# The first stage of a two-block kernel: input modulated before the tables, rounds one group ahead, products with an operand in PSUM

## The chip, the cores and the metric

The kernel runs on one core of one Trainium2 chip. A core has TensorE (matrix products), VectorE, ScalarE and GpSimd, which work side by side on 128 partitions, with SyncE starting transfers; the rows call them PE, DVE, ACT, POOL and SP. Data lies in SBUF, and matrix products are written to PSUM, which the other engines can read and VectorE and ScalarE here also write. The metric is the device time of one execution in microseconds (us); less is better.

## What is computed

Two transformer-like blocks with a model width of 1024 and a sequence of 512. Only the first mixer is touched by the change. It is a modulated RMS norm, a projection, a diagonal complex state space model in 64 groups of 16 channels with 64 states each, a gelu, a gated product and an output projection:

```
def s5_mixer(h, w_in, lam_re, lam_im, log_dt, b_re, b_im, c_re, c_im, d_skip, w_glu, w_out):
    u = h @ w_in                      # h: the modulated input, 512 x 1024
    dt = exp(log_dt); mag = exp(lre * dt)
    lb = mag * cos(lim * dt), mag * sin(lim * dt)          # the discrete eigenvalue
    k = (lb - 1) / lam                                     # k_re, k_im
    bb = k * b                                             # complex, 64 states x 16 channels per group
    h[l] = lb * h[l-1] + bb @ u[l]                         # a scan over 512 steps
    y = Re(c @ h) + d_skip * u
    y = gelu(y); y = y * sigmoid(y @ w_glu)
    return y @ w_out
```

Then come a gated FFN with a convolution, an attention with forgetting, another FFN, and in the second block a further attention, its FFN and a last attention.

## The kernel before

Every fp32 product of the large projections is made as three products of parts: operands are split in a high part (`hi`) and a low part (`lo`, the rest), and `mm3` (L373 to L375) adds hi by hi, lo by hi and hi by lo. So a product of one 128-wide output slice over the whole width is 8 x 3 = 24 matmuls of 128x512.

**The start of the first stage** (0 to about 78 us). RMS norm: sums of squares come from TensorE as they arrive, `norm.sums()` turns them into a reciprocal root by a short chain on VectorE (L206 to L261, then four products `dg` at L212), `norm.spread` broadcasts it by TensorE and `rs` takes it to SBUF. `normalise(k)` (L899) multiplies the eight slices of the input by it on GpSimd. Beside that VectorE works out cosine, sine and exponential for 64 x 64 eigenvalues (`sincos`, 62 instructions), `l1r, l1i`, then `k` (`kre`, `kim`, L822 to L834); GpSimd makes eight powers of the eigenvalue (`LR`, `LI`, L805 to L814); VectorE makes larger powers (`pows`, L857 to L861) and from these the table `few` (tile `cb`, L864 to L875). The modulation `A, B` (L1114, L416) needs a small product of TensorE, which ends with the last of 32 parts of the modulation's weights. `split_x(k)` makes the eight pairs of parts of the modulated input: `hnh` on ScalarE (L909), the whole value again (tile `t`, on VectorE for odd k by the mask `V_DVE`, L911, on ScalarE for even k, L913), and `hnl` as their difference on VectorE (L914).

**Eight groups** n = 0 to 7 (of eight 16-channel groups each) then go through steps whose order is written out by hand in the string `ORDER`. VectorE, TensorE and GpSimd run in just that order; ScalarE's order is set by the scheduler, by its own estimate of when operands are there. The steps:
- `K` tables: ScalarE scales two rows of the loaded `bc`, GpSimd makes `k1, k2` = k times b (six products of 128x128, L969 to L974)
- `F` the outer product `bt` of powers and k1, k2 (`for_b`, on VectorE, six instructions of 128x512, all operands in SBUF) and `C` the outer product `cp` of powers and c (`for_c`, on GpSimd, six of 128x576; the tile `cp` has three buffers)
- `W` split of an input weight slice (`whi` on ScalarE, `wlo` on GpSimd, 128x1024; two buffers) and `G` the 24 matmuls of the projection slice
- `P` eight transposes (L1015, into two PSUM tiles `pt`, copied by ScalarE to `bp`, L1016) and eight pairs of small products (L1022, L1025) that ScalarE copies to `lags`, from which the DMAs of `A` build a Toeplitz matrix
- `L` and `U` transfers (the group's input in another layout; the rotations `ecs`), `R` six products on VectorE that make a table of rotations from `few`
- `I` eight products of input and `bp`; `S` on VectorE two products, a sum, a scan and a product; `B` on VectorE a product and a sum; `O` 32 small products (L1080, L1082), which read `cp` too
- `Y`, `v`, `a`, `b`: the first of the gated products

The line that names the positions and the buffer that ties GpSimd to TensorE are

```
Z_POOL, W_ADD, SUMS_POS, SPREAD_POS, GATE_RATE = 0, 'dve', 12, 22, 1.3
self.cp = sp.tile([P, G8, 9, 16], F32, name="cp", bufs=3)
```

`SUMS_POS` and `SPREAD_POS` say behind how many of the 32 weight parts on TensorE the two steps of the norm stand. PSUM pools: `ps_s` three buffers, `ps_t` two, `ps_a` one.

## Time and profile before

| | us |
|---|---|
| median of three runs | 2670.97 |
| the runs | 2665.52, 2674.68, 2670.97 |
| the profiled execution | 2667.51 |
| its span | 2665.7 |
| TensorE busy | 2520.3 |
| VectorE busy | 1786.4 |
| ScalarE busy | 1149.9 |
| GpSimd busy | 408.0 |
| mean granted clock of TensorE | 0.968 |

The first stage takes the first 258 us of the span. A timeline row gives start, duration, engine, line and operation, `out<-in`, shape and count, and in brackets how long the engine stood idle just before and what released it. A windows row gives for a stretch its length and then, for TensorE, its weight loads, VectorE, ScalarE and GpSimd, the busy time with the number of instructions; then the granted TensorE clock (1.00 is 2.4 GHz, 0.50 is 1.2 GHz), the share of DMA and its rate.

### The profile page before, as it was taken

What the parts mean: (1) busy time and instruction counts of PE and PEld (TensorE: products, weight loads), DVE (VectorE), ACT (ScalarE), POOL (GpSimd) and SP (SyncE); (2) the same over time, 40 slices, a digit from 0 to 9 for tenths busy, and PEclk for the clock granted to TensorE, in tenths of its full rate; (3) what the DMA queues carried; (4) which work ended last, traced back from release to release, by engine and by line L of the source; (5) the groups of instructions that cost most, each with busy time, mean ns of one, the idle gap of its engine ahead of it and who ended that gap; (6) DMA issues with size and microseconds to landing.
All of it is one profiled execution on the core that took longest, in us unless ns stands there. A gap on an engine that the chain in (4) does not pass through costs nothing. (4 is left out here: it accounts for less than half of the span.)

```text
span 2665.7 us, 32804 instructions
## 1 busy us (share of the span) xinstructions
PE 2520.3 (95%) x12098; PEld 2021.3 (76%) x12098; DVE 1786.4 (67%) x3071; ACT 1149.9 (43%) x1915; POOL 408.0 (15%) x396
## 2 busy tenths in 40 slices
...
GB/s 200 110 125 150 229 191 139 136 149 120 105 112 103 111 121 163 155 171 179 143 103 115 115 95 127 162 149 172 170 139 98 32 29 95 83 87 99 101 77 75
DMA packets 131121, 335.67 MB, mean 126 GB/s; under 512 B 37009, under 2 KB 41873, under 8 KB 130961
## 3 DMA queue, kind: packets, MB, share of 16 engines
...
## 5 line engine op out<-in xcount | busy, mean ns | idle before, releaser
L267 DVE TENSOR_TENSOR wlo<-wraw,whi 128x1024 fp32r<-128x1024 f32 (+4 forms) x424 | 465.4, 1098 | 421.4 <-ACT whi L266 415.9
L266 ACT ACTIVATE whi<-wraw 128x1024 fp32r<-128x1024 f32 (+4 forms) x431 | 408.6, 949 | 759.6 <-PE mm L374 558.3
L373 PE MATMUL mm<-hnh,whi 128*128 128x512 f32 x1152 | 467.1, 406 | 39.1 <-ACT hnh L909 29.6
L374 PE MATMUL mm<-hnl,whi 128*128 128x512 f32 x1152 | 462.9, 402 | 6.3 <-POOL hnl L291 3.9
L375 PE MATMUL mm<-hnh,wlo 128*128 128x512 f32 x1152 | 459.1, 399 | 0.1
L373 PE MATMUL mm<-g,whi 128*128 128x512 f32 (+1 forms) x922 | 359.9, 391 | 6.3 <-ACT g L266 3.1
L375 PE MATMUL mm<-g,wlo 128*128 128x512 f32 (+1 forms) x922 | 359.3, 390 | 0.0
L374 PE MATMUL mm<-g,whi 128*128 128x512 f32 (+1 forms) x922 | 358.8, 389 | 0.1
L373 PEld LDWEIGHTS mm<-hnh,whi 128*128 128x128 f32 x1152 | 219.4, 191 | 90.9 <-ACT hnh L909 29.9
L373 PE MATMUL s<-hnh,whi 128*128 128x512 f32 x720 | 288.2, 400 | 0.0
L374 PE MATMUL s<-hnl,whi 128*128 128x512 f32 x720 | 285.2, 396 | 0.0
L375 PE MATMUL s<-hnh,wlo 128*128 128x512 f32 x720 | 283.8, 394 | 0.0
L374 PEld LDWEIGHTS mm<-hnl,whi 128*128 128x128 f32 x1152 | 219.0, 190 | 63.5 <-POOL hnl L291 9.2
L375 PEld LDWEIGHTS mm<-hnh,wlo 128*128 128x128 f32 x1152 | 218.8, 190 | 50.0 <-issue 0.7
L131 DVE SCALAR_TENSOR_TENSOR ada<-ada,cb 128x1024 f32<-128x1024 f32 x192 | 239.5, 1248 | 8.3 <-DMA ada<-in_ada_w_dram 8.1
L373 PEld LDWEIGHTS mm<-g,whi 128*128 128x128 f32 x922 | 173.6, 188 | 45.4 <-ACT g L266 3.8
L374 PEld LDWEIGHTS mm<-g,whi 128*128 128x128 f32 x922 | 173.9, 189 | 37.8 <-DVE g L272 0.7
L375 PEld LDWEIGHTS mm<-g,wlo 128*128 128x128 f32 x922 | 173.8, 189 | 37.6 <-issue 0.8
L375 PEld LDWEIGHTS s<-hnh,wlo 128*128 128x128 f32 x720 | 135.2, 188 | 32.7 <-issue 0.7
L373 PEld LDWEIGHTS s<-hnh,whi 128*128 128x128 f32 x720 | 135.4, 188 | 30.2
L374 PEld LDWEIGHTS s<-hnl,whi 128*128 128x128 f32 x720 | 135.4, 188 | 29.7 <-issue 0.5
L586 ACT ACTIVATE p<-p,nb 128x128 f32<-128x128 f32 x192 | 106.0, 554 | 69.9 <-DVE nb L581 41.7
...
## 6 DMA issues: line engine op xcount, KB each, us to landing
...
```

What stands on the lines that cost most here:

```text
L131: dve.scalar_tensor_tensor(raw, raw, 1.0, cb, op0=OP.mult, op1=OP.mult, accum_out=dst[:, i:i + 1])
L266: act.activation(hi, v, AF.Copy)
L267: return eng.tensor_tensor(lo, v, hi.bitcast(F32), OP.subtract)
L373: pe.matmul(ps, wh, xh, start=start, stop=False)
L374: pe.matmul(ps, wh, xl, start=False, stop=False)
L375: return pe.matmul(ps, wl, xh, start=False, stop=stop).ins
L586: act.activation(p[:, sl], p[:, sl], AF.Exp, bias=nb[:, qb:qb + 1], scale=scale, accum_out=l[:, qb:qb + 1])
```

## The change

Four things are changed, all in the first stage.
- **The start.** `SUMS_POS` goes from 12 to 8 and `norm.sums()` stands ahead of sincos on VectorE; `SPREAD_POS` from 22 to 18, and `spread`, `rs` and the eight `normalise` stand ahead of `l1r` and the powers. `split_x` for the first two slices and the first weight split stand right behind the modulation; the table `few` is merged with the other `split_x`; the first `F` and `R` are steps of `ORDER`, behind `G0`.
- **k folded into the powers.** `KR, KI` = powers times k (six instructions of 128x512 on GpSimd, once, with temporaries in the tile name `t0`) take the place of `k1, k2` in each group (six of 128x128 on GpSimd).
- **One operand in PSUM.** b is copied by ScalarE to a PSUM tile (`bsp`), and `for_b` reads it there: two instructions of 128x512 and eight of 128x256 instead of six of 128x512, and its temporary is in PSUM too. The powers for `few` and its temporary, and in `states` and `back` the second input, the sum, the scan and the swapped copy are in PSUM. The small products of `P` read `bt` for `k1`, and both their outputs are in `pt` tiles.
- **`ORDER`.** Steps are put in another order; rounds stand one group further ahead.

```
--- before.py
+++ after.py
@@ -71,12 +71,17 @@
 C_DVE, BC_BUFS = 0, 3
-Z_POOL, W_ADD, SUMS_POS, SPREAD_POS, GATE_RATE = 0, 'dve', 12, 22, 1.3
+Z_POOL, W_ADD, SUMS_POS, SPREAD_POS, GATE_RATE = 0, 'dve', 8, 18, 1.3
 T_ACT, MERGE_AT = 0, 50
-ORDER = ("G0 K1 W1 G1 C1 P0 F1 U1 L0 I0 L1 W2 G2 W3 K2 S0 A0 F2 B0 C2 L2 R1 G3 P1 I1 O0 U2 A1 W4 K3 S1 F3 "
-         "B1 C3 L3 G4 P2 I2 O1 U3 A2 W5 K4 S2 F4 B2 C4 L4 G5 P3 I3 O2 R2 U4 A3 W6 K5 S3 F5 B3 C5 L5 P4 I4 "
-         "G6 O3 U5 A4 W7 K6 S4 F6 B4 C6 L6 G7 P5 I5 O4 R3 U6 A5 K7 S5 F7 B5 C7 L7 P6 I6 A6 P7 O5 U7 S6 B6 "
-         "I7 A7 O6 Y0 Y1 S7 B7 O7 v0 Y2 Y3 Y4 Y5 a0 a1 a2 a3 v1 a4 a5 b0 b1 b2 b3 b4 b5 Y6 Y7 a6 a7 b6 b7 ")
+ORDER = ("G0 W1 F0 G1 L0 R0 U0 P0 A0 K1 W2 C1 F1 G2 L1 I0 K2 "
+         "S0 F2 B0 U1 C2 W3 P1 A1 G3 I1 O0 R1 U2 L2 K3 "
+         "S1 F3 B1 C3 W4 P2 A2 G4 I2 O1 U3 L3 K4 "
+         "S2 F4 B2 C4 W5 P3 A3 G5 I3 O2 R2 U4 L4 K5 "
+         "S3 F5 B3 C5 W6 P4 A4 G6 I4 O3 U5 L5 K6 "
+         "S4 F6 B4 C6 W7 P5 A5 G7 I5 O4 R3 U6 L6 K7 "
+         "S5 F7 B5 C7 P6 A6 I6 O5 U7 L7 Y0 v0 Y1 "
+         "S6 Y2 B6 P7 A7 a0 a1 I7 O6 v1 Y3 "
+         "S7 Y4 B7 a2 a3 b0 b1 O7 Y5 b2 b3 a4 b4 a5 b5 Y6 Y7 a6 a7 b6 b7 ")
+
+        for i in range(BC_POS, SUMS_POS):
+            part(i)
+        act.dma_start(vec, ap["vecs"])
+        merge(ln.ops)
+        norm.sums()
...
+        for i in range(SUMS_POS, SPREAD_POS):
+            part(i)
+        rb = norm.spread(ps_mm, "mm")
+        rs = tmp.tile([P, S], F32, name="t3")
+        act.activation(rs, rb, AF.Copy)
+        hs = []
+
+        def normalise(k):
+            t = hnp.tile([P, S], F32, name="hnl")
+            pool.tensor_tensor(t, h[k], rs, OP.mult)
+            hs.append(t)
+        for k in range(KD):
+            normalise(k)
         l1r, l1i = sm("l1r"), sm("l1i")
         dve.tensor_tensor(l1r, mag, cs, OP.mult)
         dve.tensor_tensor(l1i, mag, sn, OP.mult)
...
+        KR, KI = (sc.tile([P, NG, 8], F32, name=n) for n in ("KR", "KI"))
         kre, kim, den, nre = sm("kre"), sm("kim"), sm("den"), sm("nre")
...
+        up = [ps_s.tile([P, S], F32, name="s") for _ in range(2)]
+        turn_by = [up[i // 2][:, i % 2 * 256:i % 2 * 256 + 192].rearrange("p (e g) -> p e g", e=3) for i in range(3)]
+        for x, y in zip(turn_by, pows):
+            act.activation(x, y, AF.Copy)
         few = cst.tile([P, D], F32, name="cb").rearrange("p (e g n) -> p e g n", e=2, n=8)
...
         X = []
...
@@ -955,44 +951,41 @@
                 if n == len(bcs):
                     bcs.append(load_bc(n))
                 self.bc = bc = bcs[n]
-                b1, b2, c1, c2 = (bc[:, j, :].rearrange("p (g c) -> p g c", c=16) for j in range(4))
-                self.c12 = c1, c2
-                act.activation(bc[:, 1, :], bc[:, 1, :], AF.Identity, scale=sgn[:, 1:2])
+                self.c12 = [bc[:, j, :].rearrange("p (g c) -> p g c", c=16) for j in (2, 3)]
                 act.activation(bc[:, 2, :], bc[:, 2, :], AF.Identity, scale=sgn[:, 0:1])
                 act.activation(bc[:, 3, :], bc[:, 3, :], AF.Copy, scale=-1.0)
-                sh = [P, G8, 16]
-                self.k1 = k1 = sp.tile(sh, F32, name="k1", bufs=3)
-                self.k2 = k2 = sp.tile(sh, F32, name="k2")
-                t = sp.tile(sh, F32, name="kt", bufs=1)
-                krb = kre[:, gs, None].to_broadcast(sh)
-                kib = kim[:, gs, None].to_broadcast(sh)
-                pool.tensor_tensor(k1, krb, b1, OP.mult)
-                pool.tensor_tensor(t, kib, b2, OP.mult)
-                pool.tensor_tensor(k1, k1, t, OP.add)
-                pool.tensor_tensor(k2, krb, b2, OP.mult)
-                pool.tensor_tensor(t, kib, b1, OP.mult)
-                pool.tensor_tensor(k2, k2, t, OP.subtract)
-
-            def outer(self, dst, x1, x2, re, im, eng, n, t):
-                half = [P, 4, n, 16]
...
+            def for_c(self, eng):
+                self.cp = cp = sp.tile([P, G8, 9, 16], F32, name="cp", bufs=3)
+                t = sp.tile([P, 4, 9, 16], F32, name="op", bufs=1)
+                x1, x2 = self.c12
+                half = [P, 4, 9, 16]
                     g0 = self.i * G8 + a
+                    lr, li = (x[:, g0:g0 + 4, :, None].to_broadcast(half) for x in (LR, LI))
+                    eng.tensor_tensor(cp[:, a:a + 4], lr, x1[:, a:a + 4, None, :].to_broadcast(half), OP.mult)
                     eng.tensor_tensor(t, li, x2[:, a:a + 4, None, :].to_broadcast(half), OP.mult)
-                    eng.tensor_tensor(dst[:, a:a + 4], dst[:, a:a + 4], t, OP.add)
+                    eng.tensor_tensor(cp[:, a:a + 4], cp[:, a:a + 4], t, OP.add)
 
             def for_b(self, eng):
 
-                self.bt = sp.tile([P, G8, 8, 16], F32, name="bt")
-                self.outer(self.bt, self.k1, self.k2, LR[:, :, 7::-1], LI[:, :, 7::-1], eng, 8,
+                self.bt = bt = sp.tile([P, G8, 8, 16], F32, name="bt")
+                x1, x2 = self.b12
+                half, quarter = [P, 4, 8, 16], [P, 2, 8, 16]
+                t = bsp[:, 256:512].rearrange("p (g a c) -> p g a c", g=2, a=8)
+                g0 = self.i * G8
+                for a in range(0, 8, 4):
+                    eng.tensor_tensor(bt[:, a:a + 4], KR[:, g0 + a:g0 + a + 4, ::-1, None].to_broadcast(half),
+                                      x1[:, a:a + 4, None, :].to_broadcast(half), OP.mult)
+                for a in range(0, 8, 2):
+                    eng.tensor_tensor(t, KI[:, g0 + a:g0 + a + 2, ::-1, None].to_broadcast(quarter),
+                                      x2[:, a:a + 2, None, :].to_broadcast(quarter), OP.mult)
+                    eng.tensor_tensor(bt[:, a:a + 2], bt[:, a:a + 2], t, OP.add)
...
                 self.lags = sp.tile([16, G8, P], F32, name="lags", bufs=LAG_BUFS)
                 for a in range(2):
-                    pk = (ps_t if a else ps_a).tile([16, 4, P], F32, name="pt" if a else "aux")
+                    pk = ps_t.tile([16, 4, P], F32, name="pt")
                     for g in range(4):
-                        pe.matmul(pk[:, g, :], self.k1[:, a * 4 + g, :],
+                        pe.matmul(pk[:, g, :], self.bt[:, a * 4 + g, 7, :],
                                   self.cp[:, a * 4 + g, 0:8, :].rearrange("p a b -> p (a b)"), start=True, stop=True)
                         c = slice((a * 4 + g) * 16, (a * 4 + g + 1) * 16)
                         pe.matmul(pk[:, g, 0:16], ident[:, 0:16], self.bc[:, 4, c], start=False, stop=True,
...
             sa = ps_s.tile([P, G8, 64], F32, name="s")
             for g in range(G8):
                 pe.matmul(sa[:, g, :], tab.bp[:, g, :], U[:, g, :], start=True, stop=True)
-            sb = tmp.tile([P, G8, 64], F32, name="t1")
+            sb = ps_s.tile([P, G8, 64], F32, name="s")
             for a in range(2):
                 act.activation(sb[HALF[a]], sa[HALF[1 - a]], AF.Copy)
             return sa, sb
@@ -1050,26 +1043,22 @@
 
             sa, sb = sab
             z0 = tmp.tile([P, G8, 64], F32, name="t0")
-            z1 = sb
             dve.tensor_mul(z0, sa, tab.ec)
-            dve.tensor_mul(z1, sb, tab.es)
-            (pool if Z_POOL else dve).tensor_tensor(z0, z0, z1, OP.add)
-            dve.tensor_tensor_scan(z1.rearrange("p a b -> p (a b)"), tab.d0.rearrange("p a b -> p (a b)"),
-                                   z0.rearrange("p a b -> p (a b)"), 0.0, OP.mult, OP.add)
-            zs = tmp.tile([P, G8, 64], F32, name="t2")
+            dve.tensor_mul(sb, sb, tab.es)
+            dve.tensor_tensor(sa, z0, sb, OP.add)
+            dve.tensor_tensor_scan(sa.rearrange("p a b -> p (a b)"), tab.d0.rearrange("p a b -> p (a b)"),
+                                   sa.rearrange("p a b -> p (a b)"), 0.0, OP.mult, OP.add)
             for a in range(2):
-                act.activation(zs[HALF[a]], z1[HALF[1 - a]], AF.Copy, scale=-1.0)
+                act.activation(sb[HALF[a]], sa[HALF[1 - a]], AF.Copy, scale=-1.0)
             w1 = tmp.tile([P, G8, 64], F32, name="t3")
-            dve.tensor_mul(w1, z1, tab.ec)
-            return w1, zs
+            dve.tensor_mul(w1, sa, tab.ec)
+            return w1, sb
 
         def back(tab, wz):
 
             w1, zs = wz
             dve.tensor_mul(zs, zs, tab.es)
-            if W_ADD == "pe":
-                return w1, zs
-            (pool if W_ADD == "pool" else dve).tensor_tensor(w1, w1, zs, OP.add)
+            dve.tensor_tensor(w1, w1, zs, OP.add)
             return w1,
...
         tabs, U = [], []
-
+        bsp = ps_a.tile([P, S], F32, name="aux")
         tabs.append(Tables(0))
-        for k in range(KD):
-            normalise(k)
-        lt, lc = Later(dve), Later(dve)
-        E[0] = rotations(0, lt)
-        tabs[0].for_b(lc)
-        if C_DVE & 1:
-            tabs[0].for_c(lc)
-        else:
-            tabs[0].for_c(pool)
-        n = len(lc.ops) * MERGE_AT // 100
-        merge(lt.ops, lc.ops[:n])
-        tabs[0].turns()
-        wt = split_w(0, pool if W_DVE & 256 else dve)
+        lf = Later(dve)
+        et = ps_s.tile([P, 2, NG, 4], F32, name="s")
+        lf.memset(few[:, 0, :, 0:1], 1.0)
+        lf.memset(few[:, 1, :, 0:1], 0.0)
...
+        for x, y, z, op in ((KR, kre, kim, OP.subtract), (KI, kim, kre, OP.add)):
+            sh = [P, NG, 8]
+            t = tmp.tile(sh, F32, name="t0")
+            pool.tensor_tensor(x, LR[:, :, 0:8], y[:, :, None].to_broadcast(sh), OP.mult)
+            pool.tensor_tensor(t, LI[:, :, 0:8], z[:, :, None].to_broadcast(sh), OP.mult)
+            pool.tensor_tensor(x, x, t, op)
         dve.tensor_tensor(mod00[:, 0:16].rearrange("p (j i) -> p j i", i=4), ada_ps[:, :, 0::32].rearrange("p i j -> p j i"),
                           col("ada_b", 0, 16).rearrange("p (j i) -> p j i", i=4), OP.add)
         A, B = affine(mod00, 0, 8, col("norm_g", 0, KD), "s5")
-        merge([lambda k=k: split_x(k) for k in range(KD)], lc.ops[n:])
+        split_x(0)
+        split_x(1)
+        wt = split_w(0, dve)
+        tabs[0].for_c(pool)
+        merge([lambda k=k: split_x(k) for k in range(2, KD)], lf.ops)
```

Where the order moved: GpSimd around the third `C`. Before (names carry buffer numbers; `wlo_975` is the low part of weight slice 4, `cp_1014` the fourth `cp`, of C3, whose buffer is that of the first):

```order
L267 TENSOR_TENSOR wlo_975<-wraw_770,whi_974 128x1024
L969 TENSOR_TENSOR k1_985<-sm_kre_304,bc_980 128x128
L970 TENSOR_TENSOR kt_987<-sm_kim_305,bc_980 128x128
L971 TENSOR_TENSOR k1_985<-k1_985,kt_987 128x128
L972 TENSOR_TENSOR k2_986<-sm_kre_304,bc_980 128x128
L973 TENSOR_TENSOR kt_987<-sm_kim_305,bc_980 128x128
L974 TENSOR_TENSOR k2_986<-k2_986,kt_987 128x128
L982 TENSOR_TENSOR cp_1014<-LR_120,bc_980 128x576
L983 TENSOR_TENSOR op_1015<-LI_121,bc_980 128x576
L984 TENSOR_TENSOR cp_1014<-cp_1014,op_1015 128x576
```

And GpSimd at the same place after (`wlo_850` is slice 3, `cp_1002` is C3, `wlo_1011` slice 4, `cp_1155` C4):

```order
L973 TENSOR_TENSOR cp_841<-cp_841,op_842 128x576
L272 TENSOR_TENSOR wlo_850<-wraw_639,whi_849 128x1024
L971 TENSOR_TENSOR cp_1002<-LR_120,bc_974 128x576
L972 TENSOR_TENSOR op_1003<-LI_121,bc_974 128x576
L973 TENSOR_TENSOR cp_1002<-cp_1002,op_1003 128x576
L971 TENSOR_TENSOR cp_1002<-LR_120,bc_974 128x576
L972 TENSOR_TENSOR op_1003<-LI_121,bc_974 128x576
L973 TENSOR_TENSOR cp_1002<-cp_1002,op_1003 128x576
L272 TENSOR_TENSOR wlo_1011<-wraw_746,whi_1010 128x1024
L971 TENSOR_TENSOR cp_1155<-LR_120,bc_1127 128x576
```

Before, the low part of slice 4 stands ahead of C3; after, it stands behind it, and so in each round from there on.

TensorE where it reads that low part, after (`pt_1040` is the last of P2, `mm_1058` is G4):

```order
L1015 MATMUL pt_1040<-cp_841,bt_823 16x128
L1018 MATMUL pt_1040<-bc_507,cc_87 16x16
L378 MATMUL mm_1058<-hnh_527,whi_1010 128x512
L379 MATMUL mm_1058<-hnl_528,whi_1010 128x512
L380 MATMUL mm_1058<-hnh_527,wlo_1011 128x512
```

The third matmul of G4 reads `wlo_1011`, and behind G4 stand I2 and O1. Before, I2 and O1 stood ahead of G5, which reads the low part that is made behind C3 (slice 5).

ScalarE at the modulated input, before (`t0_570` is the whole value of slice 0) and after (`t0_529` is that of slice 0, `t2_556` of slice 2; `hnl_361` and so on are the normalised slices):

```order
L909 ACTIVATE hnh_568<-hnl_517,m_ada00_132,A_s5_566 128x512
L913 ACTIVATE t0_570<-hnl_517,m_ada00_132,A_s5_566 128x512
L909 ACTIVATE hnh_575<-hnl_519,m_ada00_132,A_s5_566 128x512
L909 ACTIVATE hnh_581<-hnl_521,m_ada00_132,A_s5_566 128x512
L913 ACTIVATE t2_583<-hnl_521,m_ada00_132,A_s5_566 128x512
```

```order
L905 ACTIVATE hnh_563<-hnl_367,m_ada00_132,A_s5_525 128x512
L905 ACTIVATE hnh_572<-hnl_369,m_ada00_132,A_s5_525 128x512
L905 ACTIVATE hnh_581<-hnl_371,m_ada00_132,A_s5_525 128x512
L905 ACTIVATE hnh_590<-hnl_373,m_ada00_132,A_s5_525 128x512
L905 ACTIVATE hnh_599<-hnl_375,m_ada00_132,A_s5_525 128x512
L909 ACTIVATE t2_592<-hnl_373,m_ada00_132,A_s5_525 128x512
L909 ACTIVATE t0_529<-hnl_361,m_ada00_132,A_s5_525 128x512
L909 ACTIVATE t0_574<-hnl_369,m_ada00_132,A_s5_525 128x512
```

The whole value of slice 0 has moved from the second place to the tenth, behind all eight high parts and the whole value of slices 2 and 6. Beyond the first stage the instructions of all engines stand as before.

## Rows read from the trace of the kernel before

**Rows 1.** The page: busy time of each engine, share of the span, instructions.
```profile
PE 2520.3 (95%) x12098; PEld 2021.3 (76%) x12098; DVE 1786.4 (67%) x3071; ACT 1149.9 (43%) x1915; POOL 408.0 (15%) x396
```

**Rows 2.** Windows: three stretches of the first stage, and one stretch inside.
```profile
75.00:131.80 56.80, 49.92 (x264) 41.46 (x265) 47.59 (x51) 30.28 (x49) 31.42 (x27) 0.81 0.49 125
131.80:213.60 81.80, 70.48 (x425) 63.40 (x424) 72.61 (x65) 35.21 (x62) 58.08 (x47) 0.75 0.50 129
213.60:258.40 44.80, 38.06 (x258) 33.88 (x257) 29.95 (x32) 21.75 (x35) 12.67 (x8) 0.86 0.51 133
...
201.20:213.60 12.40, 12.31 (x64) 11.77 (x65) 9.86 (x15) 6.24 (x10) 2.79 (x4) 0.50 0.54 128
```

**Rows 3.** Timeline of TensorE: parts and sums at the start, and three waits.
```profile
11.74 9.22 PE L768 MATMUL s<-hnh,ecs 128*32 128x512 f32 x24 [11.74 <-DMA hnh<-in_ada_w_dram]
...
22.48 0.36 PE L198 MATMUL pt<-ones,sq 128*128 128x1 f32 x2
...
78.50 0.79 PE L373 MATMUL mm<-hnh,whi 128*128 128x512 f32 x1 [29.64 <-ACT hnh L909]
...
136.89 0.39 PE L1022 MATMUL pt<-cp,k 128*16 128x128 f32 x2 [2.88 <-ACT bp L1016]
...
201.29 0.61 PE L1022 MATMUL pt<-cp,k 128*16 128x128 f32 x2 [4.28 <-ACT bp L1016]
```

**Rows 4.** Timeline of VectorE and ScalarE at the start.
```profile
9.32 0.26 DVE L716 TENSOR_SCALAR t<-sm_t 128x192 f32<-128x192 f32 x1 [0.62 <-ACT sm_t L795]
...
38.38 1.33 DVE L846 TENSOR_TENSOR sm_mag<-sm_mag 128x64 f32<-128x64 f32 x3
...
45.30 0.11 DVE L864 MEMSET cb<- 128x64 f32 x1
...
61.66 0.77 DVE L716 TENSOR_TENSOR ada<-cb 128x512 f32<-128x512 f32 x1
...
77.18 0.16 DVE L1114 TENSOR_TENSOR m_ada<-pt,vec 128x16 f32<-128x16 f32 x1
...
78.35 0.80 ACT L913 ACTIVATE t<-hnl,m_ada,A_s 128x512 f32<-128x512 f32 x1
```

**Rows 5.** Timeline of TensorE: the pieces of a round, and where rounds begin.
```profile
94.70 1.04 PE L1015 MATMUL pt<-cc,bt 128*128 128x128 f32 x8
...
97.96 2.00 PE L1043 MATMUL s<-U,bp 128*128 128x64 f32 x16
...
127.68 0.39 PE L373 MATMUL mm<-hnh,whi 128*128 128x512 f32 x1
...
131.81 1.03 PE L1015 MATMUL pt<-cc,bt 128*128 128x128 f32 x8
...
185.72 0.33 PE L1080 MATMUL s<-U,T 128*128 128x64 f32 x2
...
189.21 0.48 PE L373 MATMUL mm<-hnh,whi 128*128 128x512 f32 x1
...
213.62 1.27 PE L1015 MATMUL pt<-cc,bt 128*128 128x128 f32 x5
```

**Rows 6.** Timeline of GpSimd: normalising, weight splits, and C with and without VectorE.
```profile
41.44 9.89 POOL L899 TENSOR_TENSOR hnl<-h,t 128x512 f32<-128x512 f32 x8 [0.56 <-ACT t L881]
...
95.85 2.35 POOL L267 TENSOR_TENSOR wlo<-wraw,whi 128x1024 fp32r<-128x1024 f32 x1 [3.07 <-ACT whi L266]
...
100.68 1.17 POOL L982 TENSOR_TENSOR cp<-LR,bc 128x576 f32<-128x576 f32 x1
...
125.39 1.20 POOL L982 TENSOR_TENSOR cp<-LR,bc 128x576 f32<-128x576 f32 x1 [7.35 <-PE s L1082]
...
134.93 2.79 POOL L267 TENSOR_TENSOR wlo<-wraw,whi 128x1024 fp32r<-128x1024 f32 x1
```

**Rows 7.** Timeline of VectorE beside a busy GpSimd: one operand in PSUM, then none.
```profile
101.23 0.69 DVE L1054 TENSOR_TENSOR t<-s,ecs 128x512 f32<-128x512 f32 x1 [6.57 <-ACT t L1046]
101.84 1.69 DVE L1055 TENSOR_TENSOR t<-t,ecs 128x512 f32<-128x512 f32 x1
```

46 lines of the change are left out of this document (12 added, 34 removed).

## The prediction

> **What bounds the kernel now.** I read the busy times first: TensorE is busy for 2520.3 of 2665.7 us, the next engine for 1786.4 [rows 1], so the kernel is as long as TensorE's work, its waits and the time lost at a lower clock. The change moves instructions only in the first stage, so I read that stage by windows [rows 2]: from 131.8 to 213.6 TensorE is busy for 70.5 of 81.8 us at a mean granted clock of 0.75, and before and behind that at 0.81 and 0.86. So there TensorE waits, and runs a large part of its work at 1.2 GHz. Then I read the waits and what comes after them: a wait of 4.28 us for ScalarE's copy `bp` ends at 201.29 [rows 3], and the next 12.4 us run at 0.50 [rows 2]; the first matmul waits for 29.64 us, up to 78.50, and a wait of 2.88 us ends at 136.89 [rows 3]. A wait costs its own length and then a stretch at half clock. Since the mean clock is 0.75 over four rounds, half of these 81.8 us ran at 1.2 GHz: some 10 us for each round.
>
> The pieces of a round at full clock [rows 5]: P from 94.70 to 97.96, 3.3 us; I 1.8; G 24 matmuls at (131.81 - 127.68) / 18 = 0.229, 5.5 us; O from 185.72 to 189.21, 3.5; together 14.1. At 131.81, G0 to G3, P0, P1, I0, I1 and O0 are done; at 213.62, four rounds later, G7, P5, I5 and O4. So a round takes (213.62 - 131.81) / 4 = 20.45 us, 6.3 more than its pieces. I work out three terms: when the first of these places is reached, how long the four rounds take, and what follows to 258.4.
>
> **The start.** Before, VectorE runs without a gap from 9.32, through sincos, k and the norm's sums (until 38.38), to the last power at 45.30; then come `few` (16.4 us, to 61.66) and the first rotations, half of F0 and the first weight's low part (15.5 us, to 77.18), then the modulation, and 1.3 us later the first matmul [rows 3, 4]. After, these 31.9 us stand behind the first matmul. But the sums now stand ahead of sincos and need TensorE's sums of squares: twelve parts take 9.22 us from 11.74, the sums' products end at 22.84, so with eight parts they end 4 x 9.22 / 12 = 3.1 earlier, at 19.8 [rows 3]. VectorE's series begins there instead of at 9.32: 10.5 us later, and the last power at about 55.8 instead of 45.30. Normalising on GpSimd (9.89 us [rows 6]) now lies beside sincos instead of beside `few`; I count the disturbance even. First matmul: 55.8 + 1.3, about 57, some 21 us earlier.
>
> Most of that is lost again. The whole value of slice 0 stands tenth in ScalarE's queue, since its buffers (`t0`) are held by the temporaries of KR and KI: ten times 0.7 us (one of 0.80 overlaps the next by a little [rows 4]) gives about 65 before VectorE can make the first `hnl`, and behind that instruction all of VectorE's work is queued. Then VectorE has the first weight's low part (2.4), `few` (16.4 before beside GpSimd; with an operand in PSUM I take 9) and ten instructions of `split_x` at 0.65: G0 ends at about 84, G1 at 91 to 94, where before it ended at 94.70 [rows 5]. F0, R0, the transfer of the rotations, F1, S0, F2 and B0 follow one another on VectorE until O0. F has ten instructions where it had six: two of 128x512 and eight of half that width, each between 0.35 and 0.69, so 4.2 to 6.9 us; I take 4.7, near the width, since a product with an operand in PSUM took 0.69 beside a busy GpSimd and one without 1.69 [rows 7]. R keeps its operands in SBUF and stays disturbed. From 84: F0 to 88, R0 to 98, F1 to 103, S0 to 108 to 110, F2 and B0 to 117, O0 to about 121. The place that stood at 131.8 comes some **10.5 us earlier**; the ends are 0 (VectorE's queue takes it all) and 21 (what the first matmul gains).
>
> **The rounds.** This is the term that decides. C waits for O three groups back, since `cp` has three buffers: C3 started at 125.39, released by the last product of O0 [rows 6]. Before, what stood behind C on GpSimd was the low part for a G that TensorE reached only after I and O of the next round. After, the low part that TensorE wants in the third matmul of the next G stands behind this C. So a round has a chain: O(n) ends, C, W, then 22 matmuls, I, O(n+1). C took 125.39 to 134.93, 9.5 us, beside VectorE, and the low part 2.79; alone, one instruction of C took 1.17 and the low part 2.35 [rows 6]. Six of 1.17 are 7.0, and the sums are a little longer: 7.3. With 0.3 for the start the chain on GpSimd is 10.0 us if VectorE leaves it alone, 12.6 if not. I take 10.0, since nearly all of VectorE's instructions there have an operand in PSUM; R, in every second round, has not.
>
> The Trainium skill, SBUF — State Buffer, section "Who interferes with whom", says that a VectorE instruction with at most one input in SBUF does not contend with GpSimd, and that one with two does. By that rule the chain is the shorter one, outside R; without it, the longer. The trace agrees on VectorE's side (0.69 against 1.69 [rows 7]); no row shows the gain on GpSimd's side.
>
> P (3.3) and two matmuls lie within these 10 us, and so does the later start of P's small products, which now wait for a buffer of `pt`. TensorE then stands for about 6 us in every round. Behind that lie 22 x 0.229 + 1.8 + 3.5 = 10.3 us of work at full clock, 20.7 at half. A wait of 6 us is longer than the three of the first stage behind which the clock fell; I take 8 us at half behind it (between the 12.4 of the row and nothing): they do 4 us of work, and the round is 10.0 + 8 + 6.3 = 24.3 us. Four rounds: 97 instead of 81.8, **15 us later**. What W, K and F save on GpSimd (k1 and k2, six instructions in each group) is off this chain.
>
> **What follows** to 258.4 is the same work, 38.1 us of TensorE in 44.8 at 0.86 [rows 2], with the first gated products put between P7, I7 and O7; the C of the last group has time. I count it 0, within 4 to either side. The powers times k cost GpSimd six instructions of 128x512, some 7 us, between the powers and C0, beside TensorE's G0, which waits for VectorE: 0.
>
> **Sum.** -10.5 + 15 + 0 = +4.5 on the profiled 2667.5, so 2672. The median of the runs lies 3.5 above the profiled execution: 2675.5, rounded to **2675**. About 0.3%, 8 us, is what a measurement here can tell from no change, so this is no change, on the slow side.
>
> **Rivals.**
> - *Faster: the clock holds.* If TensorE's wait in the rounds is shorter (the low part of the weight is not late, or C is quicker) or the clock does not fall behind it, a round is 10.0 + 10.3 = 20.3, as long as before, and the start's 10.5 remain, up to 16 if VectorE is quicker with `few` and R: 2655 to 2660. For it: VectorE's load in a round falls, and GpSimd has fewer instructions. Against it: each wait shown was followed by half clock.
> - *Slower: GpSimd's chain sets the round and each G starts at half clock.* Chain 12.6 where VectorE disturbs it, or 12 us at half: 10.0 + 12.4 + 4.1 = 26.5 and 12.6 + 8 + 6.3 = 26.9. Four rounds are then 106 to 108, 24 to 26 later: +14 to +16, about 2686; with both, 2694. From a round of 25.1 us on ((81.8 + 10.5 + 8) / 4) the kernel is slower by over 0.3%. For it: the wait comes back in each round, at the same place.
> - *The operands in PSUM don't do what they are for*, GpSimd being held up as before: that is the chain of 12.6, and F with four instructions more; 2686 too.
>
> The Trainium skill, TensorE: Matmul & The Clock Gate, section on the oscillation of the clock, tells of a loop in which a wait before each tile lets each tile start at the low clock, at every turn. By that, all four rounds pay alike, and the slower rival's 26.5 is the round; by the rows, where waits of 2.9 and 4.3 us stood in two of the four rounds, I stay at 24.3 and give that rule a part of the slower chance.
>
> **Chances.** No change (2663 to 2679) 0.40: the start's gain and the rounds' loss are of one size, but each is uncertain by 6 to 8 us. Slower 0.35: both slower rivals, with the low end of the start's gain. Faster 0.25. The range leaves out the extremes: 2655 (rounds as before, the start's gain 16) to 2694 (chain and clock both bad).
>
> **What would show it.** In the trace of the changed kernel: the first matmul at about 57, and the second only at about 66, behind VectorE's `hnl` of slice 0; O0's end at about 121; in each of four rounds GpSimd's C starting right at O's end, the weight's low part 7 to 8 us later, and TensorE's third matmul of G waiting about 6 us for it, then a clock of 0.50. If TensorE waits there for less than 2 us, the rounds are as long as before and the kernel is faster; if C's instructions still take 1.6 us, it is slower. If O0 ends later than 127, the start's term was wrong.

## The result and the profile after

The changed kernel takes 2686.8 us (median of six runs, 2682.41 to 2694.47), the kernel before 2671.41 us in six runs beside them: a ratio of 1.0062, with a 95% interval of 1.0044 to 1.008. So it is about 15 us slower. That lies inside the predicted range (2655 to 2694), but the case that I held likeliest, no change (2663 to 2679), is not what happened. The profiled execution took 2694.47 us with a span of 2692.7 and a mean granted clock of 0.965; it is the slowest of the six, 7.7 us above their median.

The page's busy times, which answer to [rows 1]:

```profile
PE 2533.7 (94%) x12098; PEld 2021.2 (75%) x12098; DVE 1733.0 (64%) x3103; ACT 1150.7 (43%) x1926; POOL 369.8 (14%) x354
```

VectorE is busy for 53 us less and GpSimd for 38 us less. TensorE, which sets the end, is busy for 13 us more in the same number of instructions: it ran slower.

**One mark has to be put right first.** The prediction says that at 131.81 in the trace of before G0 to G3 and O0 are done. That is wrong: O0 ends at 125.1 (C3, which waits for it, starts at 125.39 in [rows 6]), and the row at 127.68 [rows 5] belongs to G4, which ends at 131.81. The stretch to 213.62 therefore holds three products G, not four. The mark that stands at the same place in both kernels is the start of C3, which waits for the end of O0, and four rounds later C7, which waits for O4. I use the starts of C3 and C7, and the first matmul of the third gated slice (258.44 before) as the end of the stage:

| | start of C3 | four rounds | tail | end of stage |
|---|---|---|---|---|
| before | 125.4 | 88.6 | 44.5 | 258.4 |
| forecast, on these marks | 121.3 | 97.2 | 44.5 | 263.0 |
| after | 130.7 | 90.2 | 57.2 | 278.2 |

The forecast terms were -10.5, +15 and 0 on the wrong mark; on the right one they are -4.1, +8.6 and 0. Their sum, +4.5, is the same, because the mark's place drops out of it. Measured in the profiled executions are +5.3, +1.7 and +12.7, together +19.7. Behind the stage the two traces differ by a further 7 us (2407 and 2414), in code that is the same; the rest of the other profiled executions lies between 2403 and 2414, so I count this as scatter. The medians differ by 15.4. The marks are not special to this execution: e12 below has the same start and rounds, its profile lies at its median, and it shows 130.1 and 90.3.

Windows on these marks, which answer to [rows 2] (length, then busy time and count of TensorE, its weight loads, VectorE, ScalarE and GpSimd, granted clock, DMA share and rate). The first row is the four rounds of before, the second those of after, the third the tail of after:

```profile
125.10:213.60 88.50, 77.18 (x449) 68.80 (x450) 79.24 (x69) 39.58 (x67) 64.42 (x51) 0.75 0.50 128
...
130.40:220.70 90.30, 70.84 (x450) 58.97 (x451) 43.65 (x77) 36.70 (x66) 38.53 (x28) 0.81 0.46 116
220.70:278.20 57.50, 43.98 (x259) 37.70 (x257) 30.43 (x43) 24.30 (x41) 10.70 (x8) 0.73 0.41 111
```

In the rounds TensorE stands idle for 90.3 - 70.8 = 19.5 us, 4.9 in each round. Before, it stood for 11.3 us, 2.8 in each, but was busy for 77.2 us at 0.75: the rounds of after have longer waits and a better clock, and the two nearly cancel. In the tail the clock is 0.73, where before had 0.86, and TensorE is busy for 43.98 us on what took 38.06 [rows 2]. Of the tail's 12.7 us, 5.9 are therefore this longer busy time and 6.8 are added waits (13.5 idle, before 6.7).

**The start.** TensorE's timeline, with the waits of the start (start, duration, line, operation, and in brackets the idle time before it and its releaser):

```profile
57.88 0.80 PE L378 MATMUL mm<-hnh,whi 128*128 128x512 f32 x1 [1.35 <-ACT hnh L905]
65.66 0.80 PE L379 MATMUL mm<-hnl,whi 128*128 128x512 f32 x1 [6.98 <-DVE hnl L910]
...
123.53 0.66 PE L1069 MATMUL s<-U,T 128*128 128x64 f32 x2 [4.94 <-ACT aux L959]
```

O0, behind this last wait, as a windows row:

```profile
123.53:130.40 6.87, 6.87 (x33) 6.87 (x34) 6.73 (x10) 0.59 (x1) 0.00 (x0) 0.50 0.28 59
```

The first matmul runs at 57.88 instead of 78.50 [rows 3], and the second waits at 65.66 for `hnl`, both as forecast (57 and 66). Up to S0 the series holds to within two us: G0 ends at 83.6, F0 at 88.4, R0 at 98.2, F1 at 103.1. Then VectorE and ScalarE read:

```profile
109.71 1.23 DVE L1049 TENSOR_TENSOR_SCAN s<-d,s 128x512 f32<-128x512 f32 x1
116.55 0.69 DVE L1054 TENSOR_TENSOR t<-s,ecs 128x512 f32<-128x512 f32 x1 [5.61 <-ACT s L1052]
```

```profile
103.05 0.72 ACT L998 ACTIVATE ecs<-ecs,cc 128x512 f32<-128x512 f32 x1 [8.79 <-DMA ecs<-ada]
...
113.58 0.72 ACT L998 ACTIVATE ecs<-ecs,cc 128x512 f32<-128x512 f32 x1 [1.80 <-DMA ecs<-ada]
...
115.95 0.57 ACT L1052 ACTIVATE s<-s 64x512 f32<-64x512 f32 x1
```

The scan of S0 ends at 110.9. VectorE's next product, `w1` (L1054), starts only at 116.55, 5.61 us later, and F2, B0 and with them O0 stand behind it. It waits for ScalarE's two swapped copies (L1052). These read the same PSUM tile as `w1`, stand ahead of it in the code, and stood in ScalarE's queue behind L998, which waited for a transfer of rotations until 113.58. The same L998 for group 0 had made ScalarE wait for 8.79 us, until 103.05.

**The rounds.** GpSimd's C and the low part behind it, which answer to [rows 6], then the waits of TensorE for the low part, and TensorE's windows from the end of each such wait to the next C:

```profile
130.73 1.16 POOL L971 TENSOR_TENSOR cp<-LR,bc 128x576 f32<-128x576 f32 x1 [23.97 <-PE s L1071]
...
133.09 1.40 POOL L973 TENSOR_TENSOR cp<-cp,op 128x576 f32<-128x576 f32 x1
...
138.18 2.35 POOL L272 TENSOR_TENSOR wlo<-wraw,whi 128x1024 fp32r<-128x1024 f32 x1
```

```profile
140.59 0.50 PE L380 MATMUL mm<-hnh,wlo 128*128 128x512 f32 x1 [1.95 <-POOL wlo L272]
...
162.76 0.79 PE L380 MATMUL mm<-hnh,wlo 128*128 128x512 f32 x1 [3.82 <-POOL wlo L272]
...
184.66 0.79 PE L380 MATMUL mm<-hnh,wlo 128*128 128x512 f32 x1 [1.36 <-POOL wlo L272]
...
207.49 0.79 PE L380 MATMUL mm<-hnh,wlo 128*128 128x512 f32 x1 [3.45 <-POOL wlo L272]
```

```profile
140.59:152.93 12.34, 12.34 (x73) 10.97 (x74) 1.56 (x3) 4.63 (x10) 0.01 (x1) 0.86 0.53 124
162.76:174.82 12.06, 12.06 (x73) 10.82 (x74) 5.50 (x9) 4.03 (x8) 0.00 (x0) 0.88 0.49 116
184.66:197.65 12.99, 12.99 (x73) 11.46 (x74) 3.73 (x8) 4.75 (x10) 0.00 (x0) 0.81 0.49 120
207.49:220.97 13.48, 13.48 (x73) 11.84 (x74) 5.51 (x9) 4.72 (x7) 0.00 (x0) 0.78 0.66 164
```

C takes 130.73 to 138.18, 7.45 us where before took 9.5 [rows 6], and the low part 2.35: the chain is 9.8 us, forecast 10.0. TensorE's third matmul of G waits for it in each of four rounds, but for 1.95, 3.82, 1.36 and 3.45 us, not 6. Part of the time went to the small products of P, which wait for ScalarE's copies of `bp` (1.34 us in the first of these rounds). Each round falls in two: 9.8 us from the start of C to that third matmul, in which all of TensorE's idle time lies, and 12.1 to 13.5 us behind it, in which TensorE has no gap and the clock is 0.78 to 0.88.

**The tail.** TensorE's waits behind the start of C7, and ScalarE and VectorE there:

```profile
226.21 0.61 PE L1015 MATMUL pt<-cp,bt 128*16 128x128 f32 x2 [4.49 <-ACT bp L1009]
...
236.55 0.66 PE L1069 MATMUL s<-U,T 128*128 128x64 f32 x2 [4.25 <-issue]
...
278.18 0.50 PE L378 MATMUL mm<-hnh,whi 128*128 128x512 f32 x1 [1.45 <-ACT t L1188]
```

```profile
218.58 1.28 ACT L126 ACT_TABLE_LOAD   x1 [2.13 <-DMA cb<-in_c_dram]
```

```profile
230.17 1.27 DVE L983 TENSOR_TENSOR bt<-KR,aux 128x512 f32<-128x512 f32 x2
...
235.03 0.69 DVE L1060 TENSOR_TENSOR s<-s,ecs 128x512 f32<-128x512 f32 x1
```

P6 waits 4.49 us for `bp`, which ScalarE makes behind `cb`, two table loads and the copies of S5. `cb` is here the conditioning vector that later modulations read; its transfer takes the buffer of the table `few`, is issued at 212.4, as R3 has read that table for the last time, and ScalarE waits for it until 218.58. O5 waits 4.25 us; it needs B5, and on VectorE B5 (L1060, at 235.03) stands behind F7 (from 230.17), which nobody wants yet.

### The profile page after: what moved, and what is told of

It reads as the page before. It is cut to its first block, busy times and chain, and to the rows that moved or that the text cites. A ratio compares the mean times of both kernels' runs of the same rounds, so it can differ in the third digit from the quotient of the medians.

```text
span 2692.7 us, 32810 instructions
## 1 busy us (share of the span) xinstructions
PE 2533.7 (94%) x12098; PEld 2021.2 (75%) x12098; DVE 1733.0 (64%) x3103; ACT 1150.7 (43%) x1926; POOL 369.8 (14%) x354
## 5 line engine op out<-in xcount | busy, mean ns | idle before, releaser
L379 PE MATMUL mm<-hnl,whi 128*128 128x512 f32 x1152 | 466.7, 405 | 15.1 <-DVE hnl L910 9.7
L380 PE MATMUL mm<-hnh,wlo 128*128 128x512 f32 x1152 | 463.7, 403 | 15.1 <-POOL wlo L272 10.6
L591 ACT ACTIVATE p<-p,nb 128x128 f32<-128x128 f32 x192 | 105.6, 552 | 70.1 <-DVE nb L586 41.9
```

Source lines behind the costliest of these rows:

```text
L379: pe.matmul(ps, wh, xl, start=False, stop=False)
L380: return pe.matmul(ps, wl, xh, start=False, stop=stop).ins
L591: act.activation(p[:, sl], p[:, sl], AF.Exp, bias=nb[:, qb:qb + 1], scale=scale, accum_out=l[:, qb:qb + 1])
```

## The experiments

The theory was that the loss lies in the new order, at three places where a queue that runs in order holds something urgent behind something that can wait: `W` behind `C` on GpSimd, `w1` behind the copies, `B5` behind `F7`. The rivals: that the operands in PSUM bring nothing or cost something, that waits taken away come back elsewhere, or that the rotations' transfer sets the pace whatever the order. The new start and the folded k have no run of their own; e5 carries both. Ratios are to the kernel before, with 95% intervals.

**W ahead of C (e1).** In four rounds of `ORDER`:

```
-         "S1 F3 B1 C3 W4 P2 A2 G4 ...
+         "S1 F3 B1 W4 C3 P2 A2 G4 ...
```

> The changed kernel with one thing moved: in the four rounds the low part of the next weight slice stands ahead of C on GpSimd (W4 C3, W5 C4, W6 C5, W7 C6). Theory GpSimd's chain: TensorE's waits for that low part (1.95, 3.82, 1.36 and 3.45 us in the changed kernel) go, and the four rounds, 22.2, 21.9, 22.8 and 23.3 us from one start of C to the next, fall to 20.5 or less; 7 to 9 us less than the changed kernel, about 2679. Rival, ScalarE's queue and the waits for the copies bp set the rounds: the waits move to bp, the rounds stay at 22 or more, and the time stays within 3 us of the changed kernel's 2687.

Measured: 2664.47 us, 0.9987 (0.9977 to 0.9998). Start of C7 (C3 starts at 130.50), and the window of the four rounds:

```profile
197.97 1.17 POOL L971 TENSOR_TENSOR cp<-LR,bc 128x576 f32<-128x576 f32 x1 [8.43 <-issue]
```

```profile
130.30:197.90 67.60, 62.67 (x452) 55.24 (x451) 45.91 (x81) 35.88 (x67) 36.55 (x27) 0.90 0.52 133
```

The start is as in after. The four rounds take 67.5 us instead of 90.2, 16.9 each, at a clock of 0.90 instead of 0.81. The idle time falls from 19.5 to 4.9 us, and the busy time from 70.8 to 62.7 for the same matmuls. So a chain on GpSimd that shows as waits of 1.4 to 3.8 us costs 5.7 us in each round. This one swap is worth 22 us in the medians, where I expected 7 to 9, and more than the whole loss.

**Temporaries of KR and KI in another buffer (e3).** `t0` becomes `t3`, so that ScalarE's whole value of slice 0 needn't wait for GpSimd:

```
-            t = tmp.tile(sh, F32, name="t0")
+            t = tmp.tile(sh, F32, name="t3")
```

> The changed kernel with the temporaries of the powers times k in the tile name t3 instead of t0, so that the whole value of slice 0 stands second instead of tenth in ScalarE's queue. TensorE's second matmul follows at about 59.5 instead of 65.66. Theory that the delay is carried on by VectorE's queue: G0 ends some 5 us earlier, the first O some 5 us earlier than 130.4, total 2681 to 2683. Rival, that it is swallowed by GpSimd beside VectorE (C0 and the second low part, until 74.8) and by the transfer of the rotations: G0 ends 1 to 3 us earlier, the total within 2 us of 2687.

Measured: 2689.36 us, 1.007 (1.0056 to 1.0084). TensorE's second matmul, a later wait, and ScalarE ahead of it:

```profile
59.63 0.80 PE L379 MATMUL mm<-hnl,whi 128*128 128x512 f32 x1 [1.27 <-DVE hnl L910]
...
227.06 0.60 PE L1015 MATMUL pt<-cp,bt 128*16 128x128 f32 x2 [9.33 <-ACT bp L1009]
```

```profile
218.48 1.28 ACT L126 ACT_TABLE_LOAD   x1 [4.25 <-DMA cb<-in_c_dram]
```

The wait of 6.98 us ahead of the second matmul is 1.27 and C3 starts at 124.92, 5.8 us earlier. But the rounds (92.1) and the tail (62.0) give back 6.7. The scheduler had put ScalarE's steps in another order, and TensorE waits for copies of `bp` for up to 9.33 us. In the tail ScalarE also stands before `cb` until 218.48, as in after until 218.58, so what C7 was earlier is lost there. The wait at the start is what I said it was; its removal alone is worth nothing here, which is near the rival's time, but not by the rival's way.

**w1 ahead of the copies (e4).** In `states`:

```
+            w1 = tmp.tile([P, G8, 64], F32, name="t3")
+            dve.tensor_mul(w1, sa, tab.ec)
             for a in range(2):
                 act.activation(sb[HALF[a]], sa[HALF[1 - a]], AF.Copy, scale=-1.0)
-            w1 = tmp.tile([P, G8, 64], F32, name="t3")
-            dve.tensor_mul(w1, sa, tab.ec)
```

> The changed kernel with the product w1 of each group written ahead of ScalarE's two swapped copies of the scan, which read the same PSUM tile, so that VectorE's w1 and the F behind it no longer wait for them. Theory that this new wait makes the first O late and the tail long: VectorE's wait of 5.61 us ahead of w1 at 116.55 goes, the first O starts at about 118 instead of 123.5 and ends at 122 to 125 instead of 130.4; in the tail the O that waited 4.25 us at 236.55 waits 1 to 2; the rounds stay as they are. Together 8 to 12 us less than the changed kernel: 2675 to 2679. Rival, that the chain of GpSimd and the transfers set those places anyway: less than 3 us.

Measured: 2677.89 us, 1.0033 (1.002 to 1.0046).

```profile
110.84 0.69 DVE L1052 TENSOR_TENSOR t<-s,ecs 128x512 f32<-128x512 f32 x1
```

```profile
122.45 1.17 POOL L971 TENSOR_TENSOR cp<-LR,bc 128x576 f32<-128x576 f32 x1 [15.70 <-PE s L1071]
```

`w1` follows the scan without a wait, and C3 starts at 122.45 instead of 130.73. Against after the kernel gains 9 us. So the wait of 5.61 us came from the place of `w1` in the code, not from the data. The rounds (88.9) and the tail (58.9) stay as they were; the tail's O5 no longer waits, as expected, but P6 waits 6.26 us for `bp`. O0 takes 3.9 us here and 6.9 in after, where it runs at 0.50 behind the wait of 4.94: so the 8.3 us are 5 of wait and 3 of clock.

**The old order with the new operands (e5), and with w1 first too (e6).** `ORDER` is that of before, with `F0 R0 U0` put behind `G0`, since they are steps of it now; e6 adds the edit of e4.

```
+ORDER = ("G0 F0 R0 U0 K1 W1 G1 C1 P0 F1 U1 L0 I0 L1 W2 G2 W3 K2 S0 A0 F2 B0 C2 ...
```

> The changed kernel (start, powers times k, operands in PSUM) with the order of steps of the kernel before, and F0, R0 and U0 put behind G0, where that order did not have them. Theory that the order of the rounds and of the tail is what loses: the four rounds take 82 us or less and the tail 45, as in the kernel before, with the start as in the changed kernel or a little later: 2668 to 2674. Rival, that the operands in PSUM (copies on ScalarE, VectorE's new wait behind them) lose it: 2682 to 2690.

> The kernel of e5 (the change with the old order of rounds) with w1 ahead of ScalarE's swapped copies. Theory that the wait behind the copies costs wherever F and B follow the scan on VectorE: 3 to 6 us less than e5's 2659.5, about 2655. Rival, that in the old order F and B have time: within 2 us of e5.

Measured: 2659.52 us, 0.9961 (0.9948 to 0.9973), and 2657.8, 0.9958 (0.9946 to 0.9971). C3 and C7 of e5:

```profile
124.40 1.17 POOL L966 TENSOR_TENSOR cp<-LR,bc 128x576 f32<-128x576 f32 x1 [14.37 <-PE s L1066]
...
193.41 1.17 POOL L966 TENSOR_TENSOR cp<-LR,bc 128x576 f32<-128x576 f32 x1 [10.11 <-ACT s L1034]
```

With its order undone, the rest of the change (start, k in the powers, operands in PSUM) makes the kernel faster, by about 10 us. Its rounds take 69.0 us, 19.6 less than before, where the theory had 82. Its tail takes 53.1, 8.6 more than before, where the theory had 45: so the order is not the whole of the tail's loss. In time the new `ORDER` costs 1.0062 - 0.9961, 1.0%, some 27 us, and that is the whole loss and more. In the old order `w1` is worth 1.7 us, within the intervals, as the rival had it.

**Both swaps in the new order (e7).** e1 and e4 together.

> The changed kernel with both edits of e1 (low part ahead of C) and e4 (w1 ahead of the copies). If the chain of GpSimd in the rounds and VectorE's new wait at the first O are two separate losses, both gains add: 2664.5 less 8 to 9, about 2656, with the first O's end at 122 and rounds of 17 us. Rival, that both take away the same wait: 2662 to 2665.

Measured: 2653.31 us, 0.9935 (0.9921 to 0.9949); C3 at 122.43, rounds 65.8, tail 53.5. Together they are worth 33.5 us, about the sum of the two gains (22 and 9), so these were two separate losses. With the two swaps the new order is as good as the old one or a little better (0.9935 against 0.9958; the intervals touch).

**Before, with only `states` and `back` in PSUM (e8).** The kernel before, with the second input, the sum, the scan and the swapped copy in PSUM, and `w1` ahead of the copies:

```
-            sb = tmp.tile([P, G8, 64], F32, name="t1")
+            sb = ps_s.tile([P, G8, 64], F32, name="s")
...
-            z1 = sb
...
-            dve.tensor_mul(z1, sb, tab.es)
-            (pool if Z_POOL else dve).tensor_tensor(z0, z0, z1, OP.add)
+            dve.tensor_mul(sb, sb, tab.es)
+            dve.tensor_tensor(sa, z0, sb, OP.add)
...
```

> The kernel before with one part of the change alone: second input, sum, scan and swapped copy of the states in PSUM (w1 ahead of the copies, so that it does not wait for them). VectorE's instructions there take 0.69 instead of up to 1.8 us beside GpSimd. Theory that operands in PSUM are what shortens a round from 20.5 to 17 us in e5: two to four us less in each of four rounds, 2657 to 2663 in all. Rival, that the outer products F, which stay in SBUF here, are what disturbs GpSimd and VectorE, or that the order decides: within 3 us of the kernel before's 2669.

Measured: 2661.95 us, 0.9974 (0.9963 to 0.9985).

```profile
119.78 1.17 POOL L982 TENSOR_TENSOR cp<-LR,bc 128x576 f32<-128x576 f32 x1 [4.19 <-PE s L1078]
...
201.04 1.17 POOL L982 TENSOR_TENSOR cp<-LR,bc 128x576 f32<-128x576 f32 x1 [3.47 <-PE s L1078]
```

C3 starts 5.6 us earlier than before and the rounds take 81.3 us, 7.3 less; the tail (52.1) takes 7.6 back. These operands in PSUM alone are a gain.

**b in SBUF for F (e9).** Everything as in after, but ScalarE's copy of b goes to an SBUF tile, so the products of F have both inputs in SBUF:

```
-                act.activation(bsp[:, 0:128], bc[:, 0, :], AF.Copy)
+                act.activation(bs[:, 0:128], bc[:, 0, :], AF.Copy)
...
```

> The changed kernel with the two rows of b that F reads copied to SBUF instead of PSUM: the two products of 128x512 and four of 128x256 in each F then have both operands in SBUF, the four sums keep one in PSUM. Theory that this operand frees GpSimd: C's six instructions, 7.45 us in the changed kernel, take 8.5 to 9.5 again, and since the low part behind them sets the round, four rounds are 4 to 8 us longer: 2691 to 2695. Rival, that F and C do not overlap in time in the changed order or don't disturb each other: C stays at 7.5 and the total within 2 us of 2687.

Measured: 2696.65 us, 1.0103 (1.009 to 1.0117). GpSimd in the first round, VectorE's F1 at the start, and TensorE and ScalarE in the tail:

```profile
135.87 1.17 POOL L971 TENSOR_TENSOR cp<-LR,bc 128x576 f32<-128x576 f32 x1 [26.08 <-PE s L1071]
...
140.71 1.61 POOL L972 TENSOR_TENSOR op<-LI,bc 128x576 f32<-128x576 f32 x1
142.40 1.74 POOL L973 TENSOR_TENSOR cp<-cp,op 128x576 f32<-128x576 f32 x1
144.10 2.52 POOL L272 TENSOR_TENSOR wlo<-wraw,whi 128x1024 fp32r<-128x1024 f32 x1
```

```profile
101.27 3.47 DVE L983 TENSOR_TENSOR bt<-KR,bs 128x512 f32<-128x512 f32 x2
```

```profile
240.40 0.61 PE L1015 MATMUL pt<-cp,bt 128*16 128x128 f32 x2 [12.48 <-ACT bp L1009]
```

```profile
231.83 1.28 ACT L126 ACT_TABLE_LOAD   x1 [6.40 <-DMA cb<-in_c_dram]
```

The instructions of C that run beside F take 1.61 and 1.74 us, the others still 1.16 and 1.40; C takes 8.23 instead of 7.45 (8.5 to 9.5 expected). On VectorE the products of F that run beside GpSimd take 2.5 to 4.6 times as long (the pair 3.47 us instead of 1.27, a half-width one 1.06 to 1.99 instead of 0.43), and F1 takes 10.2 us instead of 4.9. In the profiled executions the rounds grow by only 1.1 us, where 4 to 8 were expected; C3 starts 5.1 us later, by this second way, and the tail is 8.9 longer, nearly all of it in P6's wait for `bp`, 12.48 us instead of 4.49, behind a longer wait of ScalarE for `cb`. So GpSimd shows in the rounds with 1.1 us only, the smaller part of the 10 us lost in the medians.

**B5 ahead of F7, on e7 (e10) and on after alone (e12).**

```
-         "S5 F7 B5 C7 P6 A6 ...
+         "S5 B5 F7 C7 P6 A6 ...
```

> The kernel of e7 with B5 ahead of F7 on VectorE in the tail (S5 B5 F7 C7 instead of S5 F7 B5 C7). Theory that the tail is long because O5 stands behind F7 on VectorE and TensorE has nothing else there (waits of 4.49 and 4.25 us at 226 and 237 in the changed kernel): O5 starts 3 to 5 us earlier and the tail, 53.5 us in e7 from the start of the last C to the third gated slice, falls to 49 to 51; 2 to 4 us less than e7's 2653. Rival, that ScalarE's queue (its wait for the last rotations' transfer) sets the tail: within 2 us of e7.

> The changed kernel with that edit alone, B5 ahead of F7. Theory as in e10: TensorE's wait of 4.25 us at 236.55 ahead of O5 falls to under 1.5, the tail of 57.2 us to 51 to 54, 3 to 6 us less than 2687. Rival, ScalarE: the wait moves to the copies bp of P7, the total stays within 2 us.

Measured: e10 2647.94 us, 0.9917 (0.9904 to 0.993), against e7's 2653.31. e12 2686.66 us, 1.006 (1.0047 to 1.0074), as after. The wait ahead of O5 in each (first e10, with the end of B5 on VectorE, then e12):

```profile
194.45 0.69 DVE L1061 TENSOR_TENSOR t<-t,s 128x512 f32<-128x512 f32 x1
...
195.24 0.66 PE L1069 MATMUL s<-U,T 128*128 128x64 f32 x2 [2.35 <-ACT ecs L998]
```

```profile
229.59 0.66 PE L1069 MATMUL s<-U,T 128*128 128x64 f32 x2 [1.19 <-ACT s L1039]
```

In e12 the wait falls from 4.25 to 1.19 us and the tail from 57.2 to 53.0. That is 0.16% of the time; with intervals of 0.14% (e12) and 0.18% (after) to either side the total neither shows nor excludes it. Of the 4.2 us only 3.1 are O5's; P6's wait, ahead of the step that was moved, is 1.4 us shorter too.

On e7 the same edit is worth 5.4 us in the medians (tail 53.5 to 49.9), though the two intervals overlap, and not by the way that I expected. O5 waits 2.65 us in e7 and 2.35 in e10. In e10 it starts as B5's sum ends, at 195.1; B5 waits there 4.64 us for ScalarE's second swapped copy. The row names L998, but that had ended at 194.8, and e14, which has no L998, shows the same 2.35 us. What goes is a wait further on: in e7 ScalarE stood 8.64 us before the transfer of the last rotations, with the copies for P7 behind it, and P7 waited 6.27 us; in e10 the scheduler has put these copies ahead of it, and P7 has no wait. So the rival's mechanism, ScalarE's queue, is what set e7's tail. First ScalarE and TensorE in e7, then ScalarE in e10:

```profile
205.68 0.72 ACT L998 ACTIVATE ecs<-ecs,cc 128x512 f32<-128x512 f32 x1 [8.64 <-DMA ecs<-ada]
...
211.18 0.58 PE L1015 MATMUL pt<-cp,bt 128*16 128x128 f32 x2 [6.27 <-ACT bp L1009]
```

```profile
203.19 0.60 ACT L1009 ACTIVATE bp<-pt 128x512 f32<-128x512 f32 x1 [0.26 <-PE pt L1008]
...
206.50 0.72 ACT L998 ACTIVATE ecs<-ecs,cc 128x512 f32<-128x512 f32 x1 [0.46 <-DMA ecs<-ada]
```

The tail of e10:

```profile
187.50:237.40 49.90, 41.93 (x256) 37.14 (x253) 28.24 (x40) 24.18 (x39) 10.71 (x8) 0.79 0.52 139
```

Its idle time, 49.9 - 41.9 = 8.0 us, is near before's 6.7; its clock is 0.79, before 0.86. e10 is faster than both kernels: 23 us below before, 39 below after.

**e7 with the temporaries of e3 (e11).**

> The kernel of e7 with the temporaries of e3, so that slice 0's whole value is second on ScalarE. In e3 the first O ended 5.5 us earlier and the gain was lost in the rounds and the tail. Theory that it was the chain of GpSimd and VectorE's wait that took it there: with these gone, 4 to 6 us of it stay, 2647 to 2650. Rival, that ScalarE's order, which the scheduler makes anew from its estimates, takes it (TensorE's waits for the copies bp grow, as in e3 with 6.02, 4.96 and 9.33 us): 2652 to 2658.

Measured: 2655.58 us, 0.9947 (0.9933 to 0.996); no gain on e7, as on after, which is the rival's time. TensorE's second matmul runs 6 us earlier, but TensorE waits for ScalarE's `lags` (1.96 us) and `bp` (3.06) before O0, and C3 starts at 123.62, no earlier than in e7; a further wait for `bp` is 7.18 us, at 214.17.

**The sign in the copies (e14).** On e10, L998 goes; its sign goes into the scale of the swapped copies, so ScalarE no longer waits for the rotations:

```
-                act.activation(self.es, self.es, AF.Identity, scale=sgn[:, 0:1])
...
-                act.activation(sb[HALF[a]], sa[HALF[1 - a]], AF.Copy)
+                act.activation(sb[HALF[a]], sa[HALF[1 - a]], AF.Copy, scale=1.0 - 2.0 * a)
...
-                act.activation(sb[HALF[a]], sa[HALF[1 - a]], AF.Copy, scale=-1.0)
...
+                act.activation(sb[HALF[a]], sa[HALF[1 - a]], AF.Copy, scale=2.0 * a - 1.0)
```

> The kernel of e10 without ScalarE's scaling of the rotations (L998), which waits in ScalarE's queue for their transfer with copies for TensorE behind it; the sign goes into the scale of the two swapped copies, so the values are the same. Theory that this wait in ScalarE's queue is what is left of the late first O and of the tail: TensorE's waits for the copies bp of 3.57 us at 107.07 and 3.46 us at 142.10 and the wait of 2.35 us for the rotations at 195.24 in e10 become shorter, the first O's end comes 2 to 4 us earlier than 122.8, total 2640 to 2645. Rival, that VectorE, which reads the rotations too, waits for the same transfers at the same time: within 2 us of e10's 2648.

Measured: 2646.35 us, 0.9919 (0.9904 to 0.9935), the same as e10.

```profile
103.63 0.28 ACT L958 ACTIVATE aux<-bc 128x128 f32<-128x128 f32 x1 [5.68 <-DVE bt L988]
...
113.79 0.40 ACT L955 ACTIVATE bc<-bc,cc 128x128 f32<-128x128 f32 x1 [2.22 <-DMA bc<-in_s_bc_dram]
```

```profile
192.33 0.66 PE L1068 MATMUL s<-U,T 128*128 128x64 f32 x2 [2.35 <-ACT s L1038]
```

The waits for `ecs` (8.79 us up to 102.95 and 0.93 in e10) are gone, but in the place of the first ScalarE waits 5.68 us for VectorE's F1, up to 103.63, and later 2.22 us for the next group's `bc`; its first copy for P1 starts at 106.39, as in e10 (106.33). So VectorE and other transfers hold it as long, near what the rival said. C3 starts at 123.01, as in e10 (122.84), though this execution's first matmul was 1.4 us later. In the rounds the wait of 3.46 us for `bp` is gone and they are 3.2 us shorter; the total doesn't show it.

The marks of all kernels together (us, from the profiled executions; medians from the timed ones):

| | C3 | rounds | tail | median |
|---|---|---|---|---|
| before | 125.4 | 88.6 | 44.5 | 2671.4 |
| after | 130.7 | 90.2 | 57.2 | 2686.8 |
| W ahead of C (e1) | 130.5 | 67.5 | 58.4 | 2664.5 |
| KR, KI in t3 (e3) | 124.9 | 92.1 | 62.0 | 2689.4 |
| w1 first (e4) | 122.5 | 88.9 | 58.9 | 2677.9 |
| old order (e5) | 124.4 | 69.0 | 53.1 | 2659.5 |
| old order, w1 (e6) | 124.0 | 65.5 | 55.8 | 2657.8 |
| W and w1 (e7) | 122.4 | 65.8 | 53.5 | 2653.3 |
| before, PSUM (e8) | 119.8 | 81.3 | 52.1 | 2662.0 |
| b in SBUF (e9) | 135.9 | 91.3 | 66.1 | 2696.7 |
| W, w1, B5 (e10) | 122.8 | 64.7 | 49.9 | 2647.9 |
| W, w1, t3 (e11) | 123.6 | 67.1 | 54.1 | 2655.6 |
| after, B5 (e12) | 130.1 | 90.3 | 53.0 | 2686.7 |
| e10, sign (e14) | 123.0 | 61.5 | 50.7 | 2646.4 |

## Why the prediction was right and wrong

- **The mark at 131.81 was misread**, as told above. The sum of the terms and the range didn't change, but their split did: with the right mark a round of before takes 22.1 us, not 20.45, so the start could gain only 4 us by my own series, not 10.5, and a round of 24.3 was 2.2 us longer, not 3.8.
- **The start: series right, one wait missed.** First and second matmul, F, R and S0 came within two us of the forecast. F takes 4.97 us (4.7 taken). The step that failed is "F2 and B0 to 117, O0 to about 121": VectorE waits 5.61 us for ScalarE ahead of `w1`, so B0 ended at 123.4, and O0 took 6.9 us at 0.50 behind TensorE's wait of 4.94, where I had counted 4. It ended at 130.4. The diff showed both lines; I had named ScalarE's queue for slice 0 only and did not ask what the copies stand behind. The Trainium skill, PSUM — Partial Sum Buffer, section on bank collisions, says that the scheduler of the compiler's back end adds a dependency between instructions on different engines that touch the same bank and the same 32 partitions of PSUM, reads too. The 5.61 us between two readers of `s` agree with it, and I had not weighed it. e4 shows the cost: without this wait C3 is at 122.45, near the 121 of the forecast. The prediction's own sign ("if O0 ends later than 127, the start's term was wrong") is what happened.
- **The rounds: chain right, the half clock behind it overestimated.** The chain of GpSimd is 9.8 us in all four rounds (10.0 forecast), and it does what the prediction says: e1, which takes the low part out of it, makes the round 16.9 us. TensorE stands for 4.9 us within it, not "about 6", but that doesn't enter the sum, since the chain ends at the same place. The step that was mis-sized is "8 us at half behind it": from the third matmul to the next C the same 10.3 us of work took 12.7 us in the mean, not 14.3, at a clock of 0.86, 0.88, 0.81 and 0.78, which is 4 to 5 us at half. So the round is 22.6 us instead of 24.3, and the term +1.7 instead of +8.6. The 8 us were reckoned from a wait "longer than the three" shown; it is longer than those of 2.88 and 4.28 us, not than the first, of 29.64 [rows 3].
- **The tail: taken at 0 within 4, measured +12.7.** This is the largest error of one term. "The C of the last group has time" holds, but I looked for GpSimd alone. TensorE waited for ScalarE's `bp` (4.49 us) and for B5 behind F7 on VectorE (4.25 us), and the stretch ran at 0.73. e12 shows the share of B5: 3.1 us of wait. P6's wait for `bp` goes with ScalarE's for the transfer of `cb`: 4.49 with 2.13 us in after, 9.33 with 4.25 in e3, 6.26 with 4.88 in e4, 12.48 with 6.40 in e9, and 0.39 with none in e10. No run moves this transfer alone, so that it is the cause is argued, not shown. The new order is only a part of the term: e5 and e8 have the old one, and tails of 53.1 and 52.1. What stays open is this, and the last 5 us: no version comes below 49.9, where before took 44.5. In e10 most of this is the lower clock (0.79 against 0.86), and none of these runs tells why.
- **The three errors** are +9.4, -7.0 and +12.7, together 15.1 us. That the median came out within 12 us of the forecast is luck in part: one error went against the other two. Against the profiled execution (2694.5, forecast 2672) it is 22.5 us off.
- **The rivals.** The slower one (a round of 26.5 to 26.9) didn't come; the kernel is slower by another way, the start and the tail. The loop in which each turn pays a wait and then half clock, from the Trainium skill, TensorE: Matmul & The Clock Gate, section on the oscillation of the clock, is seen in part: all four rounds had a wait for the low part, but behind it the clock was 0.78 to 0.88, and the round 22.6 us, not 26.5. So a wait at every turn didn't mean half clock for the whole turn. "The operands in PSUM don't do what they are for" is refuted: C took 7.45 us against 9.5, e8 gains 7 us by those of the states alone (0.26%), and e9 loses 10 when that of F is taken away. The rule of the Trainium skill, SBUF — State Buffer, "Who interferes with whom", held on both sides: beside F with both inputs in SBUF, GpSimd's instructions took 1.61 and 1.74 us; with one in PSUM 1.16 and 1.40.
